# One transformer layer in fp32 on one core: when adaLN rows are added, where the last modulation stands, and when column sums are finished

## The chip, the core and the metric

The kernel runs on one core of a Trainium2 chip. The metric is device time in microseconds (us) of one execution, as the median of several runs. The core has a matrix engine (PE, with a weight-load part PEld), a vector engine (DVE), a scalar engine (ACT), a pool engine (POOL) and a queue that issues transfers (SP). Each of them takes its instructions in the order in which they were put down when the program was built; the transfers themselves run on 16 DMA engines.

## What is computed

One layer over 256 tokens of width 2048: a SwiGLU feed-forward block, a token mixer (forgetting attention and mLSTM heads), and a second feed-forward block. Nine vectors of length 2048, worked out from a condition `c`, shift, scale and gate them.

```python
ada = (jax.nn.silu(c) @ w_ada + b_ada)[:, None, :]
sh1, sc1, g1, sh2, sc2, g2, sh3, sc3, g3 = jnp.split(ada, N_ADA, axis=-1)
h = _swiglu(_modulate(x, sh1, sc1), ffn1_w_in, ffn1_w_out)
x = _layernorm(ALPHA * x + 0.5 * (1 + g1) * h, ln1_g, ln1_b)
h = _token_mixer(_modulate(x, sh2, sc2), w_in, ..., w_out)
x = _layernorm(ALPHA * x + (1 + g2) * h, ln2_g, ln2_b)
h = _swiglu(_modulate(x, sh3, sc3), ffn2_w_in, ffn2_w_out)
x = _layernorm(ALPHA * x + 0.5 * (1 + g3) * h, ln3_g, ln3_b)
```

`_modulate(x, shift, scale)` is `_layernorm(x) * (1 + scale) + shift`. The matrix `w_ada` has 2048 rows and 9 x 2048 columns in fp32, 151 MB of the 510.91 MB that the kernel moves; each weight is read once.

## The kernel before

**Weights.** Every product is made with three matmuls on split operands. A weight block of 1 MB comes by one transfer into a `raw` buffer (three of them), ACT casts it to the upper part `hi` and DVE subtracts to get the lower part `lo` (`split`, L144), into six buffers each of 1024 columns, and PE multiplies hi by hi, hi by lo and lo by hi (`mm3`, L354). Such a block is called a step here: 8 slices of 128 rows by 256 columns, times three, is 48 matmuls of 256 columns, or 24 of 512. One step follows another through the whole layer: first feed-forward input (`first_in`, `ffn_in`), its output (`out_proj`), the boundary to the mixer, the mixer's products, the mixer's output (`out_proj` again), the boundary to the second feed-forward block, its input in two halves, and its output.

**The ada vectors.** They are not made by matmuls over the weight, but by DVE: a row block of `w_ada`, 128 rows by 1024 columns (512 KB), is fetched into `araw` (two buffers), and DVE adds it, times a column of silu(c), into the accumulator `acc` (one buffer) (`ada_acc`, L156). After 16 such rows the accumulator is split in two halves one after the other (`ada_split`), and PE sums each half over the partitions (`ada_sum`, tile `bc`). `ada_pair` (L176) and `ada_gate` (L197) are generators: they yield once after each row, and yield PAUSE twice ahead of each of the two sums. 14 accumulators of 16 rows are queued this way, one behind the other; they are named here by vector and part: pair 3 and pair 6 (shift and scale of the mixer and of the last block, four parts each) and gates 2, 5 and 8 (two parts each). The first parts of the layer are served by a function of its own, `first_ada`.

**How they are spread.** After each step the kernel calls `pump(rate)` (L231). It adds the rate (1.25, 1.2, 1, 1.42, 0.9 and 0.6 rows in the stages one after another, L638) to a debt, and takes rows from the queue while the debt is 1 or more. A PAUSE ends the call without being paid for, so that the debt grows during the pauses, and the rows that it stands for are taken all at once after them. `need(n)` (L239) takes whatever is left of the first n parts of the queue.

**Order.** Which instruction stands before which on an engine is chosen by the list scheduler of the language when the program is built: it plays the program through with estimated durations, and an engine that is free takes the first in program order of the instructions that are ready by these estimates. So a row may be fetched and added ahead of its place in the program, as far as the buffers `araw` and `acc` are free. Inside some blocks the order is written out by hand: in the boundaries for DVE (`manual_schedule`, L528). In the execution this order stays: an instruction that waits holds up what stands behind it on its engine, and a transfer that waits for its buffer holds up the transfers behind it on SP.

**Late sums.** `out_proj` (L385) makes the output in column groups of 1024, 512 and 512. When a group's products are done, each of its pieces has three DVE steps left: times gate, plus residual, statistics (`add_up`, L425). They are put into `late` and worked off by `catch_up(n)`, n steps after each weight step of the next group (L391). In the mixer's output a group of 512 has only four weight steps; in the feed-forward outputs it has eleven. After the last step, `finish` runs the boundary. In the last group the products of the first token half go first, and those of the second are held back for the boundary (`held`), so that PE has something to do while DVE works on the first half.

**The last block's modulation.** The first half of the second feed-forward input (columns 0 to 1023 of the normalized input) goes while the scales of the second half are still being made. The modulated columns 1024 to 1535 (`modulate_both(6, 2, ...)`, L277) are made from step j = 7 on, and 1536 to 2047 (`modulate_both(6, 3, ...)`) from step j = 9 on, each after `need` (L1273). One `modulate_both` is two ACT operations, eight transposes on PE, and for each of four column blocks two ACT operations and one DVE subtraction. Then `cols_1024` (L611) goes through u = 4 to 7; a u has two blocks of 128 columns, so that u = 6 and 7 use what `modulate_both(6, 3, ...)` makes.

Of the kernel before, what the change touches and what calls it, by code (L numbers as in the profile page):

```python
# [17 lines left out]
KD = D // P  # L18
# [29 lines left out]
def layer_kernel(  # L48
# [127 lines left out]
    def ada_pair(v, js):  # L176
        for j in js:
            src = pair_cols(v, j)
            acc = ap.tile([P, 2, 512], F32, tag="acc", name=f"acc{v}_{j}")
            for k in range(KD):  # L180
                raw = ap.tile([P, 2, 512], F32, tag="araw", bufs=2, name=f"ar{v}_{j}_{k}")
                SP.dma_start(raw, src[k * P:(k + 1) * P])
                ada_acc(acc, raw, k)
                yield
            for i in range(2):
                parts = ada_split(acc[:, i, :], f"{v}_{j}_{i}")
                for _ in range(2):
                    yield PAUSE
                bc = ada_sum(parts, f"{v}_{j}_{i}")
                dg = ap.tile([P, 4, P], F32, tag="alo", name=f"dg{v}_{j}_{i}")  # L190
                V.tensor_tensor(out=dg, in0=bc.rearrange("p (a b) -> p a b", b=P),
                                in1=ident.unsqueeze(1).to_broadcast([P, 4, P]), op=ALU.mult)
                V.tensor_reduce(out=scsh[:, v + i, j * 4:(j + 1) * 4], in_=dg, axis=AX.X, op=ALU.add)
            cs = scsh[:, v:v + 2, j * 4:(j + 1) * 4]
            V.tensor_tensor(out=cs, in0=cs, in1=bcol[:, v:v + 2, j * 4:(j + 1) * 4], op=ALU.add)

    def ada_gate(v, s):  # L197
        for j in range(2):
            c0 = v * D + j * 1024
            acc = ap.tile([P, 1024], F32, tag="acc", name=f"acc{v}_{j}")  # L200
            for k in range(KD):
                raw = ap.tile([P, 1024], F32, tag="araw", bufs=2, name=f"ar{v}_{j}_{k}")
                SP.dma_start(raw, w_ada[0, k * P:(k + 1) * P, c0:c0 + 1024])
                ada_acc(acc, raw, k)
                yield
            G_.dma_start(gate[:, j * 1024:(j + 1) * 1024], b_ada[0:1, c0:c0 + 1024].to_broadcast([P, 1024]))
            for i in range(2):
                parts = ada_split(acc[:, i * 512:(i + 1) * 512], f"{v}_{j}_{i}")
                for _ in range(2):
                    yield PAUSE  # L210
                bc = ada_sum(parts, f"{v}_{j}_{i}")
                gs = gate[:, j * 1024 + i * 512:j * 1024 + (i + 1) * 512]
                V.scalar_tensor_tensor(out=gs, in0=bc, scalar=1.0, in1=gs, op0=ALU.add, op1=ALU.add)
                if s != 1.0:
                    V.tensor_scalar_mul(gs, gs, s)

    ada_left = {}
    PAUSE = 1
# [9 lines left out]
    parts_done = [0]  # L228
    owed = [0]

    def pump(n):  # L231
        owed[0] += n
        while owed[0] >= 1:
            if next(ada_left["g"], 0) is PAUSE:
                break
            owed[0] -= 1


    def need(n):  # L239
        while parts_done[0] < n and next(ada_left["g"], 0) != 0:  # L240
            owed[0] = 0


# [141 lines left out]
    def out_proj(w, rows, nk, tag, npump, finish, before=None, turn=0, nheld=3, spare=None):  # L385
# [5 lines left out]
        def catch_up(n):  # L391
            while n and late:
                if next(late[0], 0) == 0:
                    late.pop(0)
                else:
                    n -= 1
        for width in (1024, 512, 512):
# [40 lines left out]
            for i in range(nu):  # L438
                u = (i + turn // kn) % nu
                hs = []  # L440
                if before:
                    before(u * kn)
                keep = spare and lastg and i == nu - nheld - 1
                place, rows_ = spare() if keep else (None, rows)
                for k in range(u * kn, u * kn + kn, 2):
                    hs += rows_(k)
                for kk, hi, lo in load_w(w[u * kn * P:(u + 1) * kn * P, col:col + width], kn, width,
                                         f"{tag}o{col}_{u}", place):
                    arg = (u * kn + kk, *hs[kk], hi, lo)
                    if keep:  # L450
                        products(0, [arg])
                        kept.append(arg)
                    elif lastg and i >= nu - nheld or not lastg and i == nu - 1:
                        held.append(arg)
                    else:
                        for a in range(2):
                            products(a, [arg])
                if not lastg and i == nu - 1:

                    late += [add_up(a, bs=(b,)) for b in range(nb) for a in range(2)]  # L460
                    products(0, held)
                    catch_up(2)
                    products(1, held)
                else:
                    catch_up(2)
                if not lastg or i < nu - 4:
                    npump()
            if lastg:
                catch_up(99)
                finish(last_products, add_up, st)  # L470
            else:
                col += width
# [135 lines left out]

    def cols_1024(raws, xs, split_, load, ps, xT, npump, u0, u1):  # L611
        for a in range(2):
            for u, raw in enumerate(raws):
                for q in range(2):
                    k = 2 * u + q
                    for b in range(2):
                        PE.matmul(ps[a, b], xs[a, k], raw(q, b), start=k == 2 * u0, stop=False)
        for u in range(u0 + len(raws), u1):
            for k, hi, lo in split_.get(u) or load(u):
                for a in range(2):  # L620
                    ts_ = slice(a * P, (a + 1) * P)
                    for b in range(2):
                        bs = slice(b * 512, (b + 1) * 512)
                        mm3(ps[a, b], xT[0][:, k, ts_], xT[1][:, k, ts_], hi[:, bs], lo[:, bs],
                            k == 2 * u0, k == 2 * u1 - 1)
            npump()
# [642 lines left out]
    for j in range(2, 10):  # L1269
        if j == 8:  # L1270
            for _ in mb:
                pass
        if j in (7, 9):  # L1273
            need(5 if j == 7 else 6)
            mb = modulate_both(6, 2 if j == 7 else 3, mr2, xT)
            next(mb)
        ps = half_in(j, 0, "fh")
        for f in range(2):
            i = 2 * j + f
            S.copy(hT[:, i, :], ps[f][:, :T])  # L1280
            S.copy(hT[:, i + 16, :], ps[f][:, T:])
    for _ in mb:
        pass
    gups = {(a, g): mm_tile(f"gf{g}{a}") for a in range(2) for g in range(2)}
    cols_1024([], {}, {}, gu_load, gups, xT, at(R_B), 4, 8)
    for a in range(2):
        for g in range(2):
            V.tensor_tensor(out=part(a, g), in0=part(a, g), in1=gups[a, g], op=ALU.add)
# [63 lines left out]
```

## Time and profile before

| what | us |
|---|---|
| median of 3 runs | 1971.78 |
| lowest and highest | 1969.59 and 1976.58 |
| the profiled execution, its own time | 1967.35 |
| span of that execution in the profile | 1965.6 |

| engine | busy us | share of the span |
|---|---|---|
| PE | 1900.2 | 97% |
| PEld | 1736.7 | 88% |
| DVE | 1486.1 | 76% |
| ACT | 944.3 | 48% |

The DMA engines moved 510.91 MB in 301822 packets, a mean of 260 GB/s. In the lists of waits a line names the engine and the tile that waited, the engine and the tile that it waited for, then the total time, the number of waits and the longest. In a timeline a line has the start, the time from the first start to the last end, the engine, the line of the kernel, the operation, the tiles and their number, and in square brackets how long the engine had been idle just before, and what ended that. A matmul's own duration (276 ns for 256 columns) is longer than the distance from one to the next, since they are pipelined.

### The profile page before, as it was taken

The page shows a single profiled execution, that of the slowest core. Times are in us where ns is not written, and L with a number is a line of the kernel's source. Part 1 is how long each engine was busy: PE and PEld are TensorE (multiplying, and loading weights), DVE is VectorE, ACT ScalarE, POOL GpSimd, SP SyncE. Part 2 cuts the span into 40 slices and gives each one's busy share as a digit, 9 for nine tenths or more (in the row PEclk, how much of TensorE's full clock was granted, in tenths as well). Part 3 has the DMA queues.
Part 4 walks back from the last instruction along what each step waited for, and adds up shares of the span by engine and source line. Part 5 has one row for each costly group of instructions (what it writes and reads, how often), then busy time and mean ns, then how long its engine had stood idle before and what let it go on. Part 6 is the DMA issues. An engine that isn't in the chain of part 4 may idle for free.

```text
span 1965.6 us, 32416 instructions
## 1 busy us (share of the span) xinstructions
PE 1900.2 (97%) x13201; PEld 1736.7 (88%) x13201; DVE 1486.1 (76%) x1827; ACT 944.3 (48%) x1328; POOL 19.6 (1%) x34
## 2 busy tenths in 40 slices
PE   3999999999999999999999999999999999999997
PEld 3999999999988888588999876899999999988886
DVE  7788888777778898678888687778756645555776
ACT  2544354443444554645755543555444444444552
POOL 0000000000000000000000000000000000000000
PEclk9999999999999999999999999999999999999998
DMA  9999878989989785589888784898757855655552
GB/s 335 333 326 315 309 234 294 310 291 303 317 297 310 269 292 199 174 302 298 268 299 287 266 276 147 293 297 296 260 194 254 278 194 187 236 191 192 193 193 86
DMA packets 301822, 510.91 MB, mean 260 GB/s; under 512 B 10819, under 2 KB 158691, under 8 KB 300649
## 3 DMA queue, kind: packets, MB, share of 16 engines
q1 hardware_dynamic: 300808, 505.70, 76.5%
q0 software_dynamic: 864, 3.15, 0.5%
q8 instruction: 103, 1.69, 0.4%
q14 instruction: 47, 0.38, 0.1%
HBM read 506.71 MB, written 2.10 MB: 259 GB/s over the span
## 4 chain that ended last, share of the span: by engine, by line
PE 77%; DMA 9%; DVE 9%; ACT 2%; issue 2%; POOL 0%; SPq 0%; DVEq 0%; ACTq 0%; POOLq 0%
PE o_f L355 8%; PE o_f L357 8%; PE o_f L356 8%; PE gu_f L355 7%; PE gu_f L357 7%; PE gu_f L356 7%; DMA ar<-in_w_ada_dram 5%; PE s L357 3%; PE s L355 3%; PE s L356 3%; DVE acc L160 2%; PE pr_f L356 2%; PE pr_f L355 2%; PE pr_f L357 2%; PE fs L355 1%
## 5 line engine op out<-in xcount | busy, mean ns | idle before, releaser
L160 DVE SCALAR_TENSOR_TENSOR acc<-ar,csil,acc 128x1024 f32<-128x1024 f32 x242 | 307.7, 1272 | 106.7 <-DMA ar<-in_w_ada_dram 105.3
L355 PE MATMUL s<-xhi_f,hi_s 128*128 128x256 f32 x768 | 213.8, 279 | 0.8 <-ACT hi_s L145 0.6
L357 PE MATMUL s<-xhi_f,lo_s 128*128 128x256 f32 x768 | 213.1, 278 | 0.6 <-DVE lo_s L146 0.5
L356 PE MATMUL s<-xlo_f,hi_s 128*128 128x256 f32 x768 | 213.4, 278 | 0.0
L357 PE MATMUL gu_f<-xhi_f,lo_f2i 128*128 128x256 f32 x768 | 212.0, 276 | 0.0
L355 PE MATMUL gu_f<-xhi_f,hi_f2i 128*128 128x256 f32 x768 | 212.0, 276 | 0.0
L356 PE MATMUL gu_f<-xlo_f,hi_f2i 128*128 128x256 f32 x768 | 212.0, 276 | 0.0
L146 DVE TENSOR_TENSOR lo_f2i<-raw_f2i,hi_f2i 128x1024 fp32r<-128x1024 f32 x96 | 116.8, 1223 | 89.5 <-ACT hi_f2i L145 89.5
L355 PE MATMUL gu_f<-xhi_f,hi_f1i 128*128 128x256 f32 x640 | 176.8, 276 | 0.2 <-DVE hT L740 0.2
L357 PE MATMUL gu_f<-xhi_f,lo_f1i 128*128 128x256 f32 x640 | 176.7, 276 | 0.0
L356 PE MATMUL gu_f<-xlo_f,hi_f1i 128*128 128x256 f32 x640 | 176.7, 276 | 0.0
L145 ACT CAST hi_f2i<-raw_f2i 128x1024 fp32r<-128x1024 f32 x96 | 100.4, 1049 | 133.7 <-PE gu_f L356 112.4
L355 PEld LDWEIGHTS s<-xhi_f,hi_s 128*128 128x128 f32 x768 | 145.1, 189 | 1.1 <-ACT hi_s L145 0.7
L357 PEld LDWEIGHTS s<-xhi_f,lo_s 128*128 128x128 f32 x768 | 144.9, 189 | 1.1 <-DVE lo_s L146 1.1
L356 PEld LDWEIGHTS s<-xlo_f,hi_s 128*128 128x128 f32 x768 | 145.2, 189 | 0.3 <-DVE xlo_f L297 0.3
L356 PEld LDWEIGHTS gu_f<-xlo_f,hi_f2i 128*128 128x128 f32 x768 | 144.1, 188 | 0.2
L355 PEld LDWEIGHTS gu_f<-xhi_f,hi_f2i 128*128 128x128 f32 x768 | 144.1, 188 | 0.2
L145 ACT CAST hi_s<-raw_s 128x1024 fp32r<-128x1024 f32 x96 | 97.3, 1050 | 97.5 <-DMA raw_s<-in_ffn_w_in_dram 56.6
L357 PEld LDWEIGHTS gu_f<-xhi_f,lo_f2i 128*128 128x128 f32 x768 | 144.1, 188 | 0.0
L146 DVE TENSOR_TENSOR lo_f2o<-raw_f2o,hi_f2o 128x1024 fp32r<-128x1024 f32 x88 | 107.7, 1224 | 44.9 <-ACT hi_f2o L145 44.8
L355 PE MATMUL o_f<-hi_f2o,hh 128*128 128x512 f32 (+1 forms) x368 | 139.4, 379 | 0.0
L357 PE MATMUL o_f<-hi_f2o,hl 128*128 128x512 f32 (+1 forms) x368 | 138.7, 377 | 0.0
(451 smaller groups left out, 5342.0 us busy)
## 6 DMA issues: line engine op xcount, KB each, us to landing
ar<-in_w_ada_dram SPq DMA_DIRECT2D x288, 512.0 KB, 5.7
raw_s<-in_ffn_w_in_dram SPq DMA_DIRECT2D x48, 1024.0 KB, 6.0
raw_f2i<-in_ffn_w_in_dram SPq DMA_DIRECT2D x48, 1024.0 KB, 5.1
raw_f1o<-in_ffn_w_out_dram SPq DMA_DIRECT2D x44, 1024.0 KB, 6.9
raw_f2o<-in_ffn_w_out_dram SPq DMA_DIRECT2D x44, 1024.0 KB, 5.1
raw_f1i<-in_ffn_w_in_dram SPq DMA_DIRECT2D x40, 1024.0 KB, 7.7
raw_mxo<-in_w_out_dram SPq DMA_DIRECT2D x16, 1024.0 KB, 6.8
raw_fh<-in_ffn_w_in_dram SPq DMA_DIRECT2D x16, 1024.0 KB, 7.5
```

The lines of the kernel that those rows point to most:

```text
L145: S.copy(hi, src)
L146: V.tensor_tensor(out=lo, in0=src, in1=hi.bitcast(F32), op=ALU.subtract)
L160: V.scalar_tensor_tensor(out=acc, in0=raw, scalar=csil[:, k:k + 1], in1=acc, op0=ALU.mult, op1=ALU.add)
L355: PE.matmul(o, ah, bh, start=start, stop=False)
L356: PE.matmul(o, ah, bl, start=False, stop=False)
L357: return PE.matmul(o, al, bh, start=False, stop=stop)
```

## The change

It has three parts.

1. A row's transfer and its addition are parted. The generators put the row into a list `landing` and yield; the next `pump` first adds what is in the list, and then fetches at most two rows, however large the debt. After the last row of an accumulator the generator yields PAUSE, so that the split comes in the next `pump`.
2. The modulation of columns 1536 to 2047, and the `need(6)` in front of it, move from step j = 9 into `cols_1024`: it starts ahead of u = 5 and is finished ahead of u = 6.
3. In `out_proj`, for groups with four steps or fewer, `catch_up` takes three steps instead of two after a weight step, except in the last group, where all that is left waits until after the last split. This concerns the mixer's output only.

```diff
@@ ada_pair (ada_gate likewise)
                 SP.dma_start(raw, src[k * P:(k + 1) * P])
-                ada_acc(acc, raw, k)
-                yield
+                landing.append((acc, raw, k))
+                yield PAUSE if k == KD - 1 else None
@@ pump, need
+    landing = []
+
+    def add_landed():
+        while landing:
+            ada_acc(*landing.pop(0))
+
     def pump(n):
+        add_landed()
         owed[0] += n
-        while owed[0] >= 1:
+        while owed[0] >= 1 and len(landing) < 2:
             if next(ada_left["g"], 0) is PAUSE:
                 break
             owed[0] -= 1
...
     def need(n):
         while parts_done[0] < n and next(ada_left["g"], 0) != 0:
+            add_landed()
             owed[0] = 0
@@ out_proj
                     catch_up(2)
                     products(1, held)
-                else:
+                elif nu > 4:
                     catch_up(2)
+                elif not lastg:
+                    catch_up(3)
                 if not lastg or i < nu - 4:
                     npump()
             if lastg:
                 catch_up(99)
+                add_landed()
                 finish(last_products, add_up, st)
@@ cols_1024
-    def cols_1024(raws, xs, split_, load, ps, xT, npump, u0, u1):
+    def cols_1024(raws, xs, split_, load, ps, xT, npump, u0, u1, before=None):
...
         for u in range(u0 + len(raws), u1):
+            if before:
+                before(u)
             for k, hi, lo in split_.get(u) or load(u):
@@ second feed-forward block
-        if j in (7, 9):
-            need(5 if j == 7 else 6)
-            mb = modulate_both(6, 2 if j == 7 else 3, mr2, xT)
+        if j == 7:
+            need(5)
+            mb = modulate_both(6, 2, mr2, xT)
             next(mb)
...
-    for _ in mb:
-        pass
+    def last_features(u):
+        if u == 5:
+            need(6)
+            mb.append(modulate_both(6, 3, mr2, xT))
+            next(mb[0])
+        if u == 6:
+            for _ in mb[0]:
+                pass
+
+    mb = []
     gups = {(a, g): mm_tile(f"gf{g}{a}") for a in range(2) for g in range(2)}
-    cols_1024([], {}, {}, gu_load, gups, xT, at(R_B), 4, 8)
+    cols_1024([], {}, {}, gu_load, gups, xT, at(R_B), 4, 8, last_features)
```

More of the change, by code (lines that the diff above doesn't have):

```diff
@@ L203, in ada_gate @@
                 SP.dma_start(raw, w_ada[0, k * P:(k + 1) * P, c0:c0 + 1024])
-                ada_acc(acc, raw, k)
-                yield
+                landing.append((acc, raw, k))
+                yield PAUSE if k == KD - 1 else None
             G_.dma_start(gate[:, j * 1024:(j + 1) * 1024], b_ada[0:1, c0:c0 + 1024].to_broadcast([P, 1024]))
```

## The prediction

> **What bounds the kernel now.** I read the page's engine totals first, then busy time by stretches, to see where PE is not busy, then the lists of waits, and last the timelines around the three longest waits that the change can reach.
>
> ```profile
> span 1965.6 us, 32416 instructions
> PE 1900.2 (97%) x13201; PEld 1736.7 (88%) x13201; DVE 1486.1 (76%) x1827; ACT 944.3 (48%) x1328; POOL 19.6 (1%) x34
> ```
>
> PE is idle for 1965.6 - 1900.2 = 65.4 us, and no change to the other engines can give more than that.
>
> ```profile
> 0.00:50.00 50.00, 18.08 (x107) 16.96 (x108) 37.89 (x53) 13.05 (x20) 2.36 (x11) 1.00 0.93 336
> 200.00:500.00 300.00, 299.55 (x2631) 298.66 (x2630) 240.65 (x270) 129.77 (x163) 0.53 (x1) 1.00 0.87 291
> 500.00:550.00 50.00, 48.19 (x366) 45.57 (x365) 42.93 (x46) 23.74 (x31) 0.00 (x0) 0.97 0.92 318
> 1150.00:1200.00 50.00, 46.26 (x221) 38.00 (x221) 40.08 (x45) 14.89 (x17) 0.61 (x1) 0.97 0.82 275
> 1200.00:1250.00 50.00, 48.85 (x213) 32.42 (x212) 34.31 (x72) 26.86 (x52) 4.18 (x7) 1.00 0.44 142
> 1300.00:1350.00 50.00, 46.46 (x343) 43.46 (x342) 40.23 (x52) 29.37 (x57) 0.00 (x0) 1.00 0.84 278
> 1950.00:1966.00 16.00, 2.80 (x24) 2.59 (x22) 10.24 (x18) 0.00 (x0) 1.52 (x1) 0.65 0.37 131
> ```
>
> The columns are the stretch, its length, busy time and instructions of PE, PEld, DVE, ACT and POOL, the granted clock, the DMA share and GB/s. The first 50 us hold 31.9 us of the idle time and the last 16 hold 13.2: start and end, which the change does not touch. That leaves 65.4 - 31.9 - 13.2 = 20.3 us for the whole middle. The stretch from 200 to 500 is what a full PE looks like: 299.55 us for 2631 matmuls, 0.1139 us each, so that one step of 48 takes 5.46 us. What ended the waits in the middle:
>
> ```profile
> PE o_mx L356 <- DVE lo_mxo L146: 3.6, 4, 1.2
> PE bc L173 <- ACT ahi L145: 3.0, 1, 3.0
> PE o_f L355 <- DVE hT L380: 1.8, 1, 1.8
> PE bc L173 <- DVE alo L146: 0.5, 1, 0.5
> ```
>
> ```profile
> DVE acc L160 <- DMA ar<-in_w_ada_dram: 105.3, 92, 3.5
> ```
>
> DVE stands still for 105.3 us behind ada rows that have not landed, 1.14 us each of 92 times. But DVE isn't the bound, and of these 105.3 us PE shows only what comes out in the four rows above: 3.6 + 3.0 + 1.8 + 0.5 = 8.9 us, 0.45% of the span. That is the size of what the change can win.
>
> **Part 1, rows added one step behind.** It adds and removes no operation: the same rows, the same additions. What it moves is the place of each addition in program order, from right behind its transfer to behind the splits and evictions of the next step. The one place where PE visibly paid for the old order is at the end of the first feed-forward input:
>
> ```profile
> 537.10 0.39 ACT L379 ACTIVATE sg_f<-gu_f 128x256 f32<-128x256 f32 x1 [1.44 <-PE gu_f L357]
> ```
>
> ```profile
> 539.65 1.28 DVE L160 SCALAR_TENSOR_TENSOR acc<-ar,csil,acc 128x1024 f32<-128x1024 f32 x1 [0.30 <-DMA ar<-in_w_ada_dram]
> 540.85 0.41 DVE L380 TENSOR_TENSOR hT<-sg_f,gu_f 128x256 f32<-128x256 f32 x1
> ```
>
> The silu was done at 537.5, but the product that frees the accumulator for PE started only at 540.85, behind a row that DVE waited 0.30 us for and added in 1.28. Put behind it, the row gives 1.58 of the 1.8 us back. Since the planner need not put it there, the ends are 0 and -1.8; I take **-1.2**, nearer the full amount because all later rows lose rank against L380.
>
> The transfers change their rhythm too. Counting the yields of the generator with the given rates, the old pumps take one or two rows a step and then five to nine at once after the pauses. The new ones take two a step for eight steps and none for four or five, whatever the rate, since the debt never gets paid off; an accumulator then takes 12 or 13 steps. In the feed-forward output and in the mixer's last stages the queue gets ahead of the old one by two to seven steps. SP shows two rows to a weight block in the old program already, because the planner runs ahead, so I put this at nothing for a steady stage, where earlier loads cover it. Where no load is ahead it has a price, which is the first rival.
>
> **Part 3, the mixer's output.** All four waits on lo_mxo are in the last group.
>
> ```profile
> 1186.57 0.39 PE L356 MATMUL o_mx<-lo_mxo,yh 128*128 128x256 f32 x1 [0.75 <-DVE lo_mxo L146]
> ```
>
> ```profile
> 1184.71 0.68 DVE L435 BATCH_NORM_STATS2 st_mx<-res 128x6 f32<-128x512 f32 x1
> 1185.31 1.20 DVE L146 TENSOR_TENSOR lo_mxo<-raw_mxo,hi_mxo 128x1024 fp32r<-128x1024 f32 x1
> 1187.42 1.23 DVE L146 TENSOR_TENSOR lo_mxo<-raw_mxo,hi_mxo 128x1024 fp32r<-128x1024 f32 x1 [0.30 <-ACT hi_mxo L145]
> 1200.40 0.43 DVE L431 TENSOR_TENSOR o_mx<-o_mx,gate 128x256 f32<-128x256 f32 x1 [5.23 <-PE o_mx L357]
> ```
>
> A late step stands in front of the split that PE waits for, and takes 0.6 us (1184.71 to 1185.31). Without them three of the four waits shrink by 0.6 each, 1.8 us; the split at 1187.42 waited for ACT instead. ACT waited for a load, and the load was late on SP:
>
> ```profile
> 1186.34 1.99 ACT L145 CAST hi_mxo<-raw_mxo 128x1024 fp32r<-128x1024 f32 x2 [4.44 <-DMA raw_mxo<-in_w_out_dram]
> ```
>
> ```profile
> 1157.72 11.31 SPq L182 DMA_DIRECT2D ar<-in_w_ada_dram  x4
> 1169.80 0.37 SPq L339 DMA_DIRECT2D raw_mxo<-in_w_out_dram  x1
> ```
>
> Four rows held the queue for 11.31 us ahead of a weight block. By the count those rows (pair 6, third part) come three steps earlier and are over before the last two groups; I give half of the other 1.8 us to that. Sum: **-2.7**, ends 0 and -3.6. The price is what is left for the end: of the 12 late steps of the first group and the 6 of the second, 5 come after the last split, 5 x 0.6 = 3.0 us, ahead of the first add_up on DVE. That one now waits 5.23 us for PE, which hides them; without that cover they would cost up to 3.0 us.
>
> **Part 2, the last scales.** The wait on ahi:
>
> ```profile
> 1324.54 0.50 PE L173 MATMUL bc<-ahi,trir 128*128 128x512 f32 x1 [3.00 <-ACT ahi L145]
> ```
>
> ```profile
> 1311.88 0.62 ACT L145 CAST ahi<-acc 128x512 fp32r<-128x512 f32 x1 [6.79 <-DVE acc L160]
> ```
>
> The last row of the fourth part of pair 6 came so late that ACT stood 6.79 us at its first half, and the second half ran into PE at 1324.54. The old program needs this part at j = 9, right after its second sum. In the new one the sums stand two to three steps of j earlier, and the first use is at u = 6, four weight steps after the old place. Both waits should go: **-3.5**, ends 0 and -3.5. No transfer is moved with it; need(6) finds nothing left in either program. What moves is the modulation, and it loses its cover:
>
> ```profile
> 1335.81 1.04 PE L287 MATMUL tp<-ident,xf 128*128 128x128 f32 x8
> ```
>
> ```profile
> 1336.73 1.06 ACT L292 ACTIVATE xf<-tp,scsh 128x256 f32<-128x256 f32 x2
> 1337.64 0.75 ACT L295 CAST xhi_f<-xf 128x256 fp32r<-128x256 f32 x2
> 1339.76 2.23 ACT L145 CAST hi_gu<-raw_gu 128x512 fp32r<-128x512 f32 x4
> ```
>
> Now the gf products of u = 4 and 5 follow the transposes and need other columns, so the chain is free. In the new program the next product needs its first block. From the start of ACT to the first xhi it is 1337.64 + 0.37 - 1336.73 = 1.28 us; if ACT starts after the fourth of eight transposes (0.52 us in), xhi is there 1.8 us after the first transpose, and the transposes take 0.8 (the next product started at 1336.61). PE waits **+1.0**. Ends: 0, if the planner slips the transposes into u = 5, and 3.2, if the four casts (2.23) stand ahead on ACT. Behind the transposes on PE stands everything else.
>
> **Sum.** -1.2 - 2.7 - 3.5 + 1.0 = -6.4 us on the profiled execution's own 1967.35 us (1.75 more than its span). That execution is 4.4 us faster than the median 1971.78 of the three runs; scaled by 1960.95 / 1967.35 the median gives **1965.4 us**, 0.32% less. About 0.3%, 5.9 us, is what a measurement of this kernel can tell from no change, so the forecast lies on that border.
>
> **Rivals.** *First: rows at the refill after the second boundary; slower.* After this boundary no weight block is ahead. The old program filled up before it took the next rows:
>
> ```profile
> 1233.01 25.88 SPq L339 DMA_DIRECT2D raw_fh<-in_ffn_w_in_dram  x8
> 1259.18 2.70 SPq L182 DMA_DIRECT2D ar<-in_w_ada_dram  x2
> 1286.37 2.70 SPq L182 DMA_DIRECT2D ar<-in_w_ada_dram  x2
> ```
>
> ```profile
> 1249.91 2.00 ACT L145 CAST hi_fh<-raw_fh 128x1024 fp32r<-128x1024 f32 x2 [2.34 <-DMA raw_fh<-in_ffn_w_in_dram]
> ```
>
> ```profile
> L355 PE MATMUL fh<-xhi_f,hi_fh x256: 276/276/366, 1241.8 to 1335.5; 128*128 128x256 f32 x128
> ```
>
> Eight blocks in 25.88 us are 3.24 us each; with a pair of rows between them four rounds took 1286.37 - 1259.18 = 27.19 us, 6.80 each, against 5.46 that PE needs. PE began fh at 1241.8 and needs the fourth block at 1241.8 + 3 x 5.46 = 1258.2; its first split was ready at about 1249.9 + 1.0 + 1.2 = 1252.1. That is 6 us ahead, of which 3 x (5.46 - 3.24) = 6.7 came from the refill: the first block had no slack. The old queue was held until the third part had been split, after the boundary; in the new one the accumulator is free before it, and the first eight rows stand ahead of the first fh block in program order. Each pair that falls into the refill then costs 6.80 - 5.46 = 1.34 us of PE. With all eight it is 10.7 us, and the late rows would keep the bc wait of 3.5 as well: -1.2 - 2.7 + 1.0 + 10.7 = +7.8, 1979.6 us. It is slower by over 0.3% from (5.9 + 2.9) / 1.34 = 6.6 pairs on. Against it: DMA is almost free during the boundary itself (142 GB/s from 1200 to 1250), and rows that go there cost nothing; with five pairs left it is +3.8, which is no change. [...]
>
> *Second: the wait of DVE and ACT on rows costs more than the four waits show; clearly faster.* All 8.9 us go and the modulation fits into u = 5; the evictions that PE waits for ahead of b_fv and b_mv gain from an ACT that stands less behind ahi:
>
> ```profile
> PE b_fv L355 <- ACT og L1144: 1.9, 1, 1.9
> PE b_mv L355 <- ACT yF L943: 1.4, 1, 1.4
> PE b_mv L355 <- ACT yM L1004: 1.3, 1, 1.3
> ```
>
> That is -8.9 - 4.6 = -13.5, 1958.3 us. Against it: these rows name no ahi.
>
> *Third: the change does not do what it says.* The planner puts rows where buffers let it, not where the pump stands; DVE has 24% idle time, so the additions may stay where they are, and the bc and lo_mxo waits come back at other places. No change, 1971.8 us.
>
> **How the numbers follow.** The forecast gets 0.47; being on the border, 0.30 of it counts as faster and 0.17 as the same. The refill gets 0.28, of it 0.18 slower (seven or eight pairs) and 0.10 the same. The clear gain gets 0.10, no effect 0.10, and 0.05 goes to slower by new waits elsewhere, since the order of everything after 300 us is planned anew. Faster 0.40, same 0.37, slower 0.23. The range goes from 1957, just under the clear gain, to 1980, just over the full refill.
>
> **What would show it.** Right: the four waits gone or below 2.5 us together; a wait of about 1 us ahead of gf's u = 6; DVE's wait on rows well below 105.3 us; PE idle between 50 and 1950 us at about 14 us. Wrong: PE waits on hi_fh or lo_fh between 1240 and 1300 with rows between the fh blocks on SP (the first rival); rows waited for as before (the third); a wait of xlo_f or hi_gu ahead of gf above 3 us.

## The result and the profile after

The changed kernel takes 1977.46 us (median of 20 runs, 1969.38 to 1981.93), the kernel before 1969.04 on the same chips (median of 20, 1960.81 to 1979.03): 1.0040 times the time, 95% interval 1.0028 to 1.0052. It is slower by 0.4%; faster by 0.3% was forecast. The profiled execution of after took 1980.7 us, 3.2 above its median, and that of before 1.7 below its own, so the two traces differ by more (13.3 us of span) than the medians (8.4).

The page of after, span and engines:

```profile
span 1978.9 us, 32421 instructions
PE 1904.7 (96%) x13201; PEld 1741.9 (88%) x13201; DVE 1484.5 (75%) x1827; ACT 945.4 (48%) x1328; POOL 18.9 (1%) x34
```

The work is the same. First by stretches, in after and then the whole middle of before (columns as in the prediction):

```profile
50.00:1950.00 1900.00, 1870.52 (x12963) 1709.03 (x12962) 1429.52 (x1747) 932.12 (x1308) 13.55 (x21) 0.99 0.77 259
500.00:550.00 50.00, 42.24 (x359) 41.31 (x357) 38.18 (x39) 20.45 (x26) 0.00 (x0) 0.95 0.88 294
1150.00:1200.00 50.00, 50.00 (x224) 40.21 (x223) 43.69 (x56) 23.10 (x37) 0.61 (x1) 1.00 0.83 278
1300.00:1350.00 50.00, 50.00 (x413) 48.77 (x413) 39.68 (x46) 30.68 (x59) 0.00 (x0) 1.00 0.92 312
1350.00:1400.00 50.00, 46.97 (x324) 42.97 (x323) 43.43 (x55) 25.50 (x36) 0.00 (x0) 0.97 0.94 312
```

```profile
50.00:1950.00 1900.00, 1879.30 (x13075) 1717.18 (x13073) 1437.92 (x1758) 931.23 (x1308) 15.70 (x22) 1.00 0.77 259
```

The two places that the change aimed at are full: the mixer's output (1150 to 1200: 50.00, before 46.26) and the scales (1300 to 1350: 50.00, before 46.46). But PE's idle time between 50 and 1950 us went up from 20.7 to 29.5 us; about 14 was forecast. The lists of waits name the new places:

```profile
PE o_f L363 <- DVE hT L388: 8.5, 1, 8.5
PE lps L977 <- DVE yl L1150: 3.1, 1, 3.1
PE o_f L364 <- DVE lo_f1o L146: 3.1, 1, 3.1
PE fs L365 <- DVE lo_fs L146: 3.0, 1, 3.0
PE bc L173 <- DVE alo L146: 0.4, 1, 0.4
```

```profile
DVE acc L160 <- DMA ar<-in_w_ada_dram: 110.1, 85, 4.1
```

Of the four old waits, those on lo_mxo and ahi are gone, that on alo is small, and that on hT is not gone but went from 1.8 to 8.5 us. Three more stand beside it that before did not have. DVE waits no less for rows (110.1 us against 105.3).

All four waits of 3 us or more have one form. The end of the first feed-forward input in after, on ACT, DVE and PE:

```profile
541.19 0.37 ACT L387 ACTIVATE sg_f<-gu_f 128x256 f32<-128x256 f32 x1
```

```profile
549.07 1.28 DVE L160 SCALAR_TENSOR_TENSOR acc<-ar,csil,acc 128x1024 f32<-128x1024 f32 x1 [2.24 <-DMA ar<-in_w_ada_dram]
550.27 0.41 DVE L388 TENSOR_TENSOR hT<-sg_f,gu_f 128x256 f32<-128x256 f32 x1
```

```profile
550.74 0.79 PE L363 MATMUL o_f<-hi_f1o,h 128*128 128x512 f32 x1 [8.50 <-DVE hT L388]
```

The silu was done at 541.6. DVE, which takes its instructions in their fixed order, still had rows and splits ahead of the product; it stood 2.24 us at a row that had not landed, and came to the product at 550.27. In the order on DVE, 13 rows of pair 3's second part stand ahead of the product that PE waits for, 11 in before: one pair more. At 704.90, late in that block's output, it is a split:

```profile
698.64 1.04 ACT L145 CAST hi_f1o<-raw_f1o 128x1024 fp32r<-128x1024 f32 x1
```

```profile
699.43 1.29 DVE L160 SCALAR_TENSOR_TENSOR acc<-ar,csil,acc 128x1024 f32<-128x1024 f32 x1 [1.97 <-DMA ar<-in_w_ada_dram]
...
703.63 2.36 DVE L146 TENSOR_TENSOR lo_f1o<-raw_f1o,hi_f1o 128x1024 fp32r<-128x1024 f32 x2
```

The upper part was ready at 699.7, the split began at 703.63, behind two rows of which the first made DVE stand 1.97 us. The turn from gf to fs is the same again:

```profile
1354.19 1.05 ACT L145 CAST hi_fs<-raw_fs 128x1024 fp32r<-128x1024 f32 x1 [3.11 <-DMA raw_fs<-in_ffn_w_in_dram]
```

```profile
1355.42 1.28 DVE L160 SCALAR_TENSOR_TENSOR acc<-ar,csil,acc 128x1024 f32<-128x1024 f32 x1 [0.51 <-DMA ar<-in_w_ada_dram]
1357.11 1.28 DVE L160 SCALAR_TENSOR_TENSOR acc<-ar,csil,acc 128x1024 f32<-128x1024 f32 x1 [0.40 <-DMA ar<-in_w_ada_dram]
1358.31 2.35 DVE L146 TENSOR_TENSOR lo_fs<-raw_fs,hi_fs 128x1024 fp32r<-128x1024 f32 x2
```

The fourth, on lps, ended at 1067.06; ahead of the splits and of the yl that PE waits for, DVE stood 2.07 us at a row:

```profile
1060.73 1.28 DVE L160 SCALAR_TENSOR_TENSOR acc<-ar,csil,acc 128x1024 f32<-128x1024 f32 x1 [2.07 <-DMA ar<-in_w_ada_dram]
```

Part 1 let rows stand one step behind their transfer, and still DVE meets rows that have not landed, with something behind them that PE needs.

**The waits are not the whole loss.** 29.5 - 20.7 = 8.8 us of idle time do not make 13.3 us of span. The rest is the clock. Stretches of 2 us behind the long wait in after, and one behind the wait of 1.8 us in before:

```profile
552.00:554.00 2.00, 2.00 (x6) 1.52 (x6) 2.00 (x4) 1.58 (x3) 0.00 (x0) 0.50 1.00 414
554.00:556.00 2.00, 2.00 (x8) 1.60 (x7) 2.00 (x3) 0.51 (x1) 0.00 (x0) 0.73 1.02 425
556.00:558.00 2.00, 2.00 (x11) 1.62 (x10) 1.01 (x3) 1.57 (x2) 0.00 (x0) 1.00 0.98 387
```

```profile
542.00:544.00 2.00, 2.00 (x6) 1.54 (x6) 2.00 (x5) 1.18 (x2) 0.00 (x0) 0.50 0.87 313
```

The column ahead of the DMA share is the granted clock. Behind the wait PE is "busy" all the time, but at half the clock it gets through 6 matmuls of 512 columns in 2 us instead of 11 (552 to 554 against 556 to 558). Summing busy time times (1 - granted clock) over such stretches from 50 to 1950 gives 11.0 us for after and 4.9 for before. With the idle time: 29.5 + 11.0 = 40.5 against 20.7 + 4.9 = 25.6, 14.9 us apart, about the 13.3 of the spans.

Not all of that belongs to the change. Up to 263 us both kernels have the same instructions in the same order on PE, DVE and ACT, and the same transfers, and yet they differ there by 3.8 us. PE waits at 177 us for a scale of the first block, in before and then in after:

```profile
177.11 0.61 PE L691 MATMUL cp<-trir,gate 128*128 128x1 f32 x4 [2.60 <-DVE scsh L693]
```

```profile
178.20 1.01 PE L704 MATMUL cp<-trir,gate 128*128 128x1 f32 x4 [4.71 <-DVE scsh L706]
```

Behind the longer wait the clock went to 0.50 (178 to 182 us), behind the shorter one it stayed at 1.00 (176 to 184). From 50 to 200 us before has 3.6 us of idle time and loses nothing to the clock; after has 5.0 and 2.4. This is scatter between executions, and most of the 4.9 us by which the traces differ more than the medians (13.3 - 8.4). The clock scatters too: the mean granted clock is 0.995 and 0.990 in the two traces, but in the median of all runs 0.993 or 0.994 for before and 0.990 for after.

### The profile page after: what moved, and what is told of

It reads as the page before. It is cut to its first block, busy times and chain, and to the rows that moved or that the text cites. A ratio compares the mean times of both kernels' runs of the same rounds, so it can differ in the third digit from the quotient of the medians.

```text
span 1978.9 us, 32421 instructions
## 1 busy us (share of the span) xinstructions
PE 1904.7 (96%) x13201; PEld 1741.9 (88%) x13201; DVE 1484.5 (75%) x1827; ACT 945.4 (48%) x1328; POOL 18.9 (1%) x34
## 3 DMA queue, kind: packets, MB, share of 16 engines
q8 instruction: 103, 1.69, 0.3%
## 4 chain that ended last, share of the span: by engine, by line
PE 70%; issue 12%; DVE 8%; DMA 7%; ACT 2%; POOL 0%; DVEq 0%; SPq 0%; ACTq 0%; POOLq 0%
PE o_f L363 8%; PE o_f L365 8%; PE o_f L364 8%; PE gu_f L364 8%; PE gu_f L363 8%; PE gu_f L365 8%; DMA ar<-in_w_ada_dram 4%; PE s L363 3%; PE s L365 3%; PE s L364 3%; DMA raw_s<-in_ffn_w_in_dram 2%; PE fs L365 1%; PE fs L363 1%; PE fs L364 1%; DVE acc L160 1%
## 5 line engine op out<-in xcount | busy, mean ns | idle before, releaser
L160 DVE SCALAR_TENSOR_TENSOR acc<-ar,csil,acc 128x1024 f32<-128x1024 f32 x242 | 308.1, 1274 | 111.1 <-DMA ar<-in_w_ada_dram 110.1
```

What stands on the lines that cost most here:

```text
L160: V.scalar_tensor_tensor(out=acc, in0=raw, scalar=csil[:, k:k + 1], in1=acc, op0=ALU.mult, op1=ALU.add)
```

## The experiments

All are timed against runs of the kernel before on the same chip. "hT" is PE's wait on the product L388 in the profiled execution; the others are the waits that changed, in us. The ratios come from all runs, the waits from one execution each.

| kernel | ratio | 95% | hT | other waits of PE |
|---|---|---|---|---|
| changed kernel | 1.0040 | 1.0028 to 1.0052 | 8.5 | lo_f1o 3.1, lps 3.1, fs 3.0 |
| part 1 | 1.0014 | 1.0001 to 1.0027 | 5.3 | lo_f1o 1.8, lps 2.9, bc 5.2 |
| part 2 | 0.9992 | 0.9975 to 1.0009 | 5.3 | o_mx 3.2, gf 0.6 |
| part 3 | 1.0012 | 0.9993 to 1.0030 | 3.0 | o_mx 2.9, bc 0.9 |
| parts 1 and 2 | 1.0061 | 1.0043 to 1.0079 | 4.9 | lo_f1o 2.4, lps 3.0, fs 3.6 |
| parts 1 and 3 | 1.0023 | 1.0006 to 1.0040 | 4.6 | lo_f1o 2.5, lps 3.0, bc 3.1 |
| parts 2 and 3 | 0.9977 | 0.9961 to 0.9993 | 2.4 | o_mx 3.8, gf 0.6 |
| rhythm without place | 1.0064 | 1.0045 to 1.0082 | 5.0 | lo_f1o 4.6, lps 3.5, fs 3.8 |
| place without rhythm | 0.9989 | 0.9975 to 1.0003 | 5.4 | o_mx 3.8, nps 2.3, gf 0.6 |
| later rows behind hT | 1.0019 | 1.0002 to 1.0035 | 0 | lo_f1o 4.4, lps 3.1, fs 4.8 |
| six pumps held back | 1.0120 | 1.0097 to 1.0143 | 0 | fs 8.0, gf 4.3, bc 4.9, o_f 3.7 |
| queue two steps later | 0.9992 | 0.9980 to 1.0004 | 2.5 | nps 3.0, bc 1.2 |
| queue four steps later | 1.0119 | 1.0099 to 1.0139 | 2.2 | fs 8.2, gf 4.3, lps 2.4 |
| late only after hT | 0.9997 | 0.9980 to 1.0013 | 7.8 | lo_f1o 0.6, bc 2.1, gf 1.0 |
| late only up to hT | 1.0007 | 0.9990 to 1.0024 | 4.4 | lo_f1o 3.0, fs 1.5 |
| parts 2 and 3, four pumps owed | 0.9963 | 0.9948 to 0.9979 | 0 | o_mx 4.8, gf 0.6 |

### Which part

Part 1 alone (the diff's hunks of `ada_pair`, `ada_gate`, `pump` and `need`; two pieces of them):

```diff
-                ada_acc(acc, raw, k)
-                yield
+                landing.append((acc, raw, k))
+                yield PAUSE if k == KD - 1 else None
...
-        while owed[0] >= 1:
+        while owed[0] >= 1 and len(landing) < 2:
```

> Part 1 alone. Theory A (the loss is the rhythm of part 1: two rows a step whatever the rate, so that one more pair of rows stands ahead of the last hT products on DVE; parts 2 and 3 win): slower than before by 0.4 to 0.8%, more than the whole change, and PE waits 6 to 10 us for hT at the start of the first feed-forward output. Theory C (the loss comes from parts 2 and 3): within 0.2% of before.

```profile
PE o_f L363 <- DVE hT L388: 5.3, 1, 5.3
PE bc L173 <- DVE alo L146: 3.2, 2, 2.6
PE lps L975 <- DVE yl L1148: 2.9, 1, 2.9
```

1.0014 (1.0001 to 1.0027): part 1 by itself is slightly slower. That is less than the 0.4 to 0.8% of theory A, and hT is below its 6 to 10 us; the time alone would also fit theory C. Part 1 brings the wait on lps and a longer one on hT, takes away the one on lo_mxo, and does nothing for bc (5.2 us with the waits on ahi).

Parts 2 and 3 in the old pump (the diff without those pieces, so that `add_landed` finds nothing):

> Parts 2 and 3 without part 1. Theory A: faster than before by 0.15 to 0.4%, the wait for hT stays at about 1.8 us, the waits on lo_mxo and ahi shrink. Theory C: slower than before by 0.3% or more.

```profile
PE o_f L363 <- DVE hT L388: 2.4, 1, 2.4
PE o_mx L364 <- DVE lo_mxo L146: 1.5, 5, 0.9
PE o_mx L364 <- DVE lo_kept L146: 1.5, 1, 1.5
```

0.9977 (0.9961 to 0.9993): faster than before, against theory C. So the loss comes in with part 1. The waits on o_mx did not shrink as expected: 3.8 us in all, 3.6 before.

Part 2 alone (the hunks of `cols_1024` and of the second block):

> Part 2 alone, with the old pump. Theory A (parts 2 and 3 each take their own waits, and only part 1 costs): the waits on ahi and alo are gone, the waits on lo_mxo stay at 3 to 4 us; 0.1 to 0.25% faster than before. Theory C (the move of the modulation costs by itself): a wait ahead of gf or fs of 2 us or more, no gain.

```profile
PE gf L363 <- ACT xhi_f L303: 0.6, 1, 0.6
```

Both waits on bc are gone, and the modulation that lost its cover costs 0.6 us, as the prediction had it (1.0). The ratio, 0.9992 (0.9975 to 1.0009), cannot tell this size from nothing.

Part 3 alone (the hunk of `out_proj`):

> Part 3 alone, with the old pump. Theory A: the waits on lo_mxo shrink by half or more, the wait on ahi stays at 3 us; 0.05 to 0.2% faster than before. Rival: the waits on lo_mxo stay, since it was the loads that were late, and the time is within 0.05%.

```profile
PE o_mx L364 <- DVE lo_mxo L146: 1.5, 5, 0.9
PE o_mx L363 <- ACT hi_mxo L145: 0.8, 1, 0.8
PE o_mx L364 <- DVE lo_kept L146: 0.6, 1, 0.6
```

Of 3.6 us of waiting 2.9 is left: where the late step went, PE now waits for the upper part, whose load is late. 1.0012 (0.9993 to 1.0030): the expected gain of 0.05 to 0.2% does not show.

Parts 1 and 2, and parts 1 and 3:

> Parts 1 and 2 without part 3. Theory D (in the new rhythm the rows of gate 8 and the moved modulation come together on DVE at the turn from gf to fs; part 3 has nothing left to win since part 1 already took the waits on lo_mxo): a wait on lo_fs or hi_fs of 2 to 4 us, no wait on lo_mxo, 0.3 to 0.5% slower than before, as the whole change. Otherwise, if part 3 is what costs beside part 1, it is like part 1 alone: 0.1 to 0.2% slower.

> Parts 1 and 3 of the change, the modulation in its old place. Theory (part 2 in the new rhythm draws the last rows and the modulation into the turn from gf to fs, where PE then waits on lo_fs): no wait on lo_fs or hi_fs at the turn, waits on bc of 3 to 5 us as with part 1 alone, ratio 1.001 to 1.003, below the 1.004 of the whole change. Rival (part 1 alone costs the whole loss and part 2 nothing; the difference of the runs so far is that between chips): 1.004 to 1.006, with no fs wait.

Parts 1 and 2, then parts 1 and 3:

```profile
PE fs L365 <- DVE lo_fs L146: 3.6, 1, 3.6
```

```profile
PE bc L173 <- DVE alo L146: 3.1, 2, 2.6
```

1.0061 (1.0043 to 1.0079) and 1.0023 (1.0006 to 1.0040). With part 1 the gain of part 2 is not there: the wait on bc (3.1 us here, 5.2 with part 1 alone) goes, and one on lo_fs (3.6) comes, at the turn from gf to fs. What stands ahead of that split on DVE is rows, two of them in parts 1 and 2 as in the lines of the whole change above; the subtractions of the moved modulation come behind it, so they are not what PE waits for, as the expectations had it. All kernels with the new rhythm from the old start show at least one of the two waits. Beside part 1, part 2 does cost: the intervals of part 1 (up to 1.0027) and of parts 1 and 2 (from 1.0043, six runs on another chip) do not overlap. With part 3 there as well, 1.0023 against 1.0040, they do.

### Place of the addition, or rhythm of the transfers

Rhythm without place: at most two rows a pump and the pause after the sixteenth, but each row added right behind its transfer.

```diff
-        while owed[0] >= 1 and len(landing) < 2:
-            if next(ada_left["g"], 0) is PAUSE:
+        left = 2
+        while owed[0] >= 1 and left:
+            got = next(ada_left["g"], 0)
+            add_landed()
+            if got is PAUSE:
                 break
+            left -= 1
```

> The change with each row added right behind its transfer again, as before, but with at most two rows a pump and the pause after the sixteenth row. Theory A (the rhythm costs, not the place of the addition): as slow as the change, 0.2 to 0.6% slower than before, the wait for hT 6 to 10 us. Theory B (adding a step later costs, since the row buffers are held longer): within 0.2% of before, the wait for hT about 2 us.

1.0064 (1.0045 to 1.0082), with all four waits of the changed kernel (hT 5.0, lo_f1o 4.6, lps 3.5, fs 3.8). The old place of the addition does not help. The wait for hT is below the 6 to 10 us of theory A, the time at its upper end.

Place without rhythm: a row is added one step behind, as far as the two buffers go, with the old debt.

```diff
-                yield PAUSE if k == KD - 1 else None
+                yield
+            add_landed()
...
-        while owed[0] >= 1 and len(landing) < 2:
+        while owed[0] >= 1:
+            if len(landing) == 2:
+                ada_acc(*landing.pop(0))
```

> The whole change, but with the old rhythm of the row transfers: no limit of two rows a pump and no pause after the sixteenth row; a row is still added one step behind its transfer, as far as the two buffers allow, and the rows still out are added ahead of the split. Theory A (the loss is the rhythm: eight steps with two rows each and then none, which shifts what the rows collide with; the place of the addition is free): as the parts 2 and 3 in the old pump, 0.998 of the kernel before (0.996 to 0.9995), hT waits near 3 us, at most 0.5 us at lps and nps. Rival B (adding a row a step behind its transfer holds the two buffers longer and costs by itself): 1.002 or above, and DVE waits less on rows than 105 us while SP stands longer in front of rows. Rival C (parts 1 and 2 collide whatever the rhythm): a wait of PE at fs on lo_fs or hi_fs of 3 us or more.

0.9989 (0.9975 to 1.0003): no loss, no wait on fs or lps. Waits on hT (5.4 us) and nps (2.3) are longer than expected, without making it slower than before. The place of the addition costs nothing that can be measured; the rhythm does. Between them these two runs settle that question for the time; the waits are those of single executions.

### What about the rhythm: the phase

Two kernels take the rows from in front of the last hT product. The first puts those from the tenth on behind it in DVE's order:

```diff
+                with tc.issue_after(hold[0].ins):
+                    ada_acc(*landing.pop(0))
...
+                last = V.tensor_tensor(out=hT[:, 2 * j + f, :], in0=sg, in1=ps[f][:, T:], op=ALU.mult)
+        if tag == "f1":
+            hold.append(last)
```

> The whole change, but the rows that are added behind the last hT product of the first feed-forward input in program order are also put behind it on DVE (rows 10 and on of pair 3's second part); no pump is left out. Theory A: the wait for hT falls from 8.5 to about 2 us or less and the time by 0.25 to 0.5% against the change: 0.0 to 0.15% slower than before. If the wait only moves to the loads behind it (the rows hold SP and lo_f1o comes late), the time stays 0.3% or more above before.

The second holds back six pumps there as well (`(lambda: None) if held_back else npump`):

> The change, but no pump in the last six weight steps before the first feed-forward output, and the additions of the rows after that put behind the last hT product on DVE. Theory A: the wait for hT falls from 8.5 to under 1 us, and the time by 8.5 and the slow-clock time behind it, about 10 us, against the change: within 0.2% of before. Theory B and C: still slower than before by 0.3% or more, whatever the wait for hT does.

Rows behind hT, then six pumps held back:

```profile
PE o_f L370 <- DVE lo_f1o L146: 4.4, 2, 3.6
```

```profile
PE fs L369 <- ACT hi_fs L145: 7.5, 1, 7.5
PE gf L369 <- ACT xhi_f L309: 4.3, 1, 4.3
```

Both take the wait on hT away. The first is at 1.0019 (1.0002 to 1.0035), between its two expectations, with the other three waits in place; the second at 1.0120 (1.0097 to 1.0143), outside both expectations: the queue is then six steps late, gf waits for the last scales, and ahead of fs ACT stands 6.45 us for a weight block that SP issued behind two of the late rows.

The queue of rows started two steps later (four: `i > 6`), nothing else changed:

```diff
-            if j == 3 and i > 2:
+            if j == 3 and i > 4:
                 pump(R_F)
```

> The whole change, with the queue of rows started two steps later in the layer; nine rows of pair 3's second part stand ahead of the last hT product on DVE by program order, not thirteen. Theory A (the wait at hT is that of rows in flight at that moment, which the rhythm shifts by steps): a row is still ahead of hT, so hT 3 to 6 us; the collisions further down (lps, lo_fs) move as well; between 1.000 and 1.005. Rival B (place of the addition costs by itself): 1.003 to 1.005 whatever the phase, with the same three waits.

> The whole change, with the queue of rows started four steps later; six rows stand ahead of the last hT product on DVE, and the new rhythm has its pause there. Theory A (phase): hT below 2.5 us, lps and nps at most 1 us in all if the pause falls elsewhere, 0.998 to 1.002. Rival B (place of the addition costs by itself): 1.003 to 1.005, with the waits at hT, lps and lo_fs as large as in the changed kernel.

Two steps, then four:

```profile
PE o_f L363 <- DVE hT L388: 2.5, 1, 2.5
```

```profile
PE fs L363 <- ACT hi_fs L145: 7.7, 1, 7.7
PE gf L363 <- ACT xhi_f L303: 4.3, 1, 4.3
```

Two steps: 0.9992 (0.9980 to 1.0004). The whole loss is gone, with the same code of parts 1 to 3; hT is at 2.5 us, and the waits on lo_f1o, lps and fs are not there. Nine rows then stand ahead of the hT product that PE waits for, not 13. Four steps: hT is at 2.2, but 1.0119 (1.0099 to 1.0139), by the late rows, as with the six pumps held back. The first is a little better than the phase theory had it and below what its rival, the place, allowed (1.003 and more). The second is outside what either expected, since both forgot the end of the queue.

Which of the collisions makes the loss? One kernel keeps the phase up to hT and is two steps late from the output on; the other is late up to hT and catches up:

```diff
+    def f1_pump():
+        calls[0] += 1
+        if calls[0] not in (5, 6):
+            pump(R_OUT)
```

```diff
-            if j == 3 and i > 2:
+            if j == 3 and i > 4:
...
+        for _ in range(1 + (calls[0] in (5, 6))):
+            pump(R_OUT)
```

> The change up to the end of the first feed-forward input, so that the same rows stand ahead of the last hT product as in the changed kernel; then the fifth and sixth pumps of its output are skipped, so that all later rows are two steps later, as in the kernel whose queue starts two steps later. Theory A1 (most of the loss is the stall at hT and what the slow clock adds to it): hT and lo_f1o together 6 to 11 us as before, the later waits as in the shifted kernel, ratio 1.002 to 1.004. Rival A2 (most of the loss is further down, at lps, nps and at the turn from gf to fs): the same hT wait, lps and fs gone, ratio 0.999 to 1.001.

> The other way round: the queue starts two steps later, so that nine rows and not thirteen stand ahead of the last hT product, and the fifth and sixth steps of the output pump twice, so that the later rows stand about where the changed kernel has them. Theory A1 (the stall at hT): hT 2 to 3 us, no wait on lo_f1o, lps and fs waits come back, ratio 0.999 to 1.001. Rival A2 (the later collisions): the same waits, ratio 1.002 to 1.004.

Late only after hT, waits and the middle; then late only up to hT:

```profile
PE o_f L363 <- DVE hT L388: 7.8, 1, 7.8
PE o_f L364 <- DVE lo_f1o L146: 0.6, 1, 0.6
```

```profile
50.00:1950.00 1900.00, 1880.34 (x13091) 1720.00 (x13090) 1438.81 (x1760) 932.75 (x1308) 15.08 (x22) 1.00 0.77 259
```

```profile
PE o_f L363 <- DVE hT L388: 4.4, 1, 4.4
PE o_f L364 <- DVE lo_f1o L146: 3.0, 2, 2.6
PE fs L365 <- DVE lo_fs L146: 1.5, 1, 1.5
```

The first has the order of the changed kernel up to 560 us and nearly the whole wait on hT, 7.8 us, and runs at 0.9997 (0.9980 to 1.0013). So the longest wait of the list does not make the loss by itself. Against it the changed kernel has 9.8 us more idle time in the middle (1880.34 - 1870.52) and, by the sum over short stretches, 11.0 - 6.2 = 4.8 us more lost to the clock: 14.6, which is what the spans differ by (1978.9 - 1964.3 = 14.6). Of these, 3.2 us lie ahead of 200 us, where both have the same order, and are scatter. The rest comes from lo_f1o, lps and fs, less what the late queue pays at bc, nps and gf. The second, 1.0007 (0.9990 to 1.0024), did not do what it was made for: lo_f1o and half of fs came back, lps did not, and hT is 4.4 where the same order had 2.5 with the queue two steps later. Its ratio lies in the range of theory A1, which the other kernel speaks against, and its interval reaches into that of A2; it decides nothing. How the 0.4% divides between the three later waits is therefore open.

### A version that is faster than both

Parts 2 and 3 with the old pump; the last four pumps of the first feed-forward input only add to the debt, and rows issued later stay behind the last hT product.

```diff
+    def owe():
+        owed[0] += R_IN
...
+                held_back = tag == "f1" and j == DFF // 256 - 1
-                            f"{tag}i{j}_{gu}", npump)
+                            f"{tag}i{j}_{gu}", owe if held_back else npump)
```

> Parts 2 and 3 in the old pump, and the last four pumps of the first feed-forward input only add to the debt; the rows from the seventh of that part on are issued after the last hT product, so the product of silu and gate stands behind fewer rows on DVE. Theory A (rows ahead of hT make PE wait, and the slow clock after the wait doubles it): hT wait of 2.4 us at most 0.5, PE 50.00 busy in 500 to 550 apart from lo_f1o, 0.2% faster than parts 2 and 3 alone: 0.9955 (0.994 to 0.998). Rival D (rows that are put off are only paid elsewhere, as in the kernel that held six pumps back in the new rhythm): hT gone but waits of about the same size at bc, fs or o_f, 0.998 or above.

On ACT and on DVE:

```profile
539.92 0.38 ACT L400 ACTIVATE sg_f<-gu_f 128x256 f32<-128x256 f32 x1 [1.44 <-PE gu_f L377]
```

```profile
540.34 0.42 DVE L401 TENSOR_TENSOR hT<-sg_f,gu_f 128x256 f32<-128x256 f32 x1 [0.60 <-ACT sg_f L400]
```

The product follows the silu at once, and PE does not wait. 0.9963 (0.9948 to 0.9979), 7.3 us faster than before. Unlike the six pumps held back, the rows are only put off: the old debt takes them later. What it adds to parts 2 and 3 alone (0.9961 to 0.9993) is not separated by the intervals.

## Why the prediction was wrong, point by point

- **The step that failed** is on part 1's transfers: the planner runs ahead in the old program too, "so I put this at nothing for a steady stage, where earlier loads cover it". The count of the new rhythm was not at fault: from 1142 to 1175 us SP has the rows in pairs, where before has four at once at 1157.72. But it was asked only whether weight blocks would be late. What became late is DVE. In a steady stage PE has loads ahead of it but not DVE's splits and products, and these stand behind rows in a fixed order. Rhythm without place costs 0.64%, place without rhythm nothing that can be measured, and two steps of phase undo the whole loss.
- **Part 1 at hT, -1.2**: the wrong sign, though 8.5 us against 1.8 overstates it. "All later rows lose rank against L380" holds for program order, but the planner put one pair more ahead of the product than before. The wait scatters: before, part 2, part 3, and parts 2 and 3 have one order on PE, DVE and ACT up to 838 us, and show 1.8, 5.3, 3.0 and 2.4 us. The changed kernel, part 1, parts 1 and 2, parts 1 and 3, and late only after hT share one up to 560 us, and show 8.5, 5.3, 4.9, 4.6 and 7.8. By the medians, 2.7 and 5.3, the new order costs 2.6 us more there.
- **Part 3, -2.7**: the wait on lo_mxo did go, but by the rows. The late steps, 1.8 of it in my sum, are worth 0.7 us of waiting and nothing in time when they alone move; with part 1 alone, no wait on lo_mxo is left. The load that came late decided, to which I had given half of the other 1.8: with part 3 alone SP still issues four rows in 11.13 us at 1161.17, with part 1 alone they come as pairs of 1.69 us. That the steps left for the end are hidden was right: no wait shows there.
- **Part 2, -3.5 + 1.0**: right in the old rhythm (bc gone, gf 0.6). Parts 2 and 3 together gave -0.23% (-0.39 to -0.07), about the -5.2 us that my sum had for them. That is luck in part, since of its -2.7 for part 3 the trace shows nothing (3.8 us of waits on o_mx). In the new rhythm the wait moved to lo_fs at the turn from gf to fs, which the sum did not have.
- **The clock** was not in the sum. It cost 4.9 us in the trace of before and 11.0 in that of after; a single trace says little of it, since part 2 alone and place without rhythm, neither slower than before, show 11.6 and 12.3. The median granted clock over all runs, 0.990 against 0.993 or 0.994, points the same way.
- **The range**, 1957 to 1980, holds the 1977.46 by luck: its upper end stood for the first rival. What happened is the 0.05 given to "slower by new waits elsewhere".
- **The second rival** failed because rows are waited for as before; **the third**, no effect, is excluded by the interval.
- **The first rival**, rows in the refill after the second boundary, fell though the result has its sign, and the range's upper end of 1980 came from it. The changed kernel's SP queue there:

```profile
1245.54 17.18 SPq L347 DMA_DIRECT2D raw_fh<-in_ffn_w_in_dram  x6
1266.62 1.69 SPq L182 DMA_DIRECT2D ar<-in_w_ada_dram  x2
```

Six blocks, 2.86 us each, went ahead of the next rows, and PE is busy for the whole 50 us from 1250 to 1300. No pair fell into the refill. The 27.19 us of before from which the 6.80 us a round are worked out ran at 315 GB/s. That is not the most that the transfers reached: in the trace of after the rows from 552 to 556 above show 414 and 425 GB/s, and the 10 us from 545 to 555 have 373.

## What to carry to other kernels

Where the instruction order of an engine is fixed, a change in how often transfers are issued must be judged at every place where that engine has something that the bound engine needs at once: list what stands ahead of it and whether it has landed. Here the loss was one of phase: try the same change a step or two earlier or later before it is judged, and look whether the end of the queue still comes in time. Only two other starts were run, two and four steps later; each also plans everything behind it anew, so whether other phases of the same rhythm are as good is not shown. Undo one wait at a time: the longest one here did not make the loss. And a wait read from one execution is one draw: with the same instruction order the wait on hT was 1.8 and 5.3 us.

## What the hardware showed beside that

Behind some waits of PE the granted clock goes to 0.50 for some microseconds, in after from about 545 to 555, 4 us beyond the wait; there that costs about 2 us more than the wait itself. It does not follow from the length of the wait alone: before had it behind the 1.81 us that ended at 541.32 (542 to 544 above), but in all the stretches of 2 us from 1322 to 1330, around the wait of 3.00 us that ended at 1324.54, the clock stayed at 1.00. What else decides it no run here shows.

Nor does it need a wait: in the kernel that is late only after hT, PE was busy without a break from 1104 to 1116 us, and the clock is 0.64 and 0.50 in the two stretches of 2 us from 1112 on; from 1112.95 to 1115.51 the products of 512 columns start 0.43 us apart, from 1116.20 on 0.23. From 1108.89 to 1112.45 PE had only small products (tile lps, 128 or 256 columns, half of them over 8 rows).
